# A decoder layer on one core: the stationary weights moved 64 bytes in SBUF, and side work reordered in the down projection and at the end

## The chip, the core and the metric

The kernel runs on one core of one Trainium2 chip. The metric is the device time of one execution in microseconds; the time before is the median of three runs, 2653.98 us (2652.39 to 2657.59).

## What is computed

One decoder layer, for 512 tokens of width 2048, in float32:

```python
q_a, k_a, v_a, q_b, k_b, v_b = jnp.split(h @ w_in[l], splits, axis=-1)
o_a = swa_sink_attention(q_a, k_a, v_a, sinks[l])      # sliding window of 128, 16 heads over 4
o_b = stick_breaking_attention(q_b, k_b, v_b)          # 16 heads, strictly causal
mix = jnp.concatenate([head_rmsnorm(o_a), head_rmsnorm(o_b)], axis=-1) @ w_o[l]
h = layer_norm(ALPHA * h + mix, ln1_g[l], ln1_b[l])
c = memory_cross_attention(h, mem, w_q_mem[l], w_kv_mem[l], w_o_mem[l])   # 4 heads, 256 keys
h = layer_norm(ALPHA * h + c, ln2_g[l], ln2_b[l])
gate, up = jnp.split(h @ w_gate_up[l], 2, axis=-1)     # 2048 -> 2 x 5632
f = (jax.nn.silu(gate) * up) @ w_down[l]
h = layer_norm(ALPHA * h + f, ln3_g[l], ln3_b[l])
```

## The kernel before, in words

**Products.** Each float32 operand is split into two float32r parts, hi and lo: ACT casts to hi (L123), DVE subtracts to get lo (L124). A product is three matmuls into the same accumulator: hi·hi, hi·lo, lo·hi (`mm3`, L144 to 149). A matmul loads its 128x128 stationary operand (PEld in the profile) while the one ahead of it streams its moving operand.

**Weights.** They come in units of 128x1024, 512 KB. `unit` (L135) loads one with a DMA on SP's queue into `ws` and splits it into `wh` and `wl`, three buffers each, in pool `pw`. `next_unit` (L683) keeps splits up to three units ahead of the product that uses them. In some stages the weights are the moving operand, with 512 columns (`v`, `wo`, `vo`, `pvo`, down); in others they are the stationary one: the attention's projections `pj..` (512 moving columns), and, with 256 moving columns, the memory's values `mvp` and keys `mkp` (`mem_project`), `kq` in the memory's attention, the early gate-up `ge`, and gate-up `zz` at L1055 (`product_turned`). Down is `zz` at L1044 (`product`).

In the built program every stationary and every moving operand of the float32r matmuls begins at the same place modulo 512 bytes. The one exception is the constant `bd`, which lies 352 bytes off that place (32 matmuls meet it: the 16 of L314 and L315 each, as the operand loaded next). The transposes are float32 and have the identity as moving operand.

**Gate-up and down** use a seven-product scheme for 2x2 blocks (Winograd's form of Strassen). A block runs through places 0 to 6, each with 2 to 4 groups; a group uses one unit. Three of the gate-up blocks are partial: part of their products was made early. The scheme's weight sums are made on DVE: `summed` adds a streamed tile to `a` or `b` (L600) and then splits it. `steps` (L575) writes the order of a block's loads and splits. Accumulators `zz` have three roles (`PRODUCTS`); places 0, 2, 4 and 6 add to the same one, and `end` (L1201) updates the four output quarters after each place. Hooks (`at_step`) put work ahead of a group.

**The end.** In the last block, `Last`, the normalisation of token tiles 0 and 1 is side work, run between the groups of the last places (`side.run`); tiles 2 and 3 follow after the loop, L1370. `shared` quarters of them go to ACT and POOL (L763 to 766), the others to DVE (L768, L770).

**Order.** PE's and SP's order is that of the code. DVE, ACT and POOL are ordered by a scheduling pass over the whole program, where `urgent` raises an operation's priority. All queues run in order.

Of the kernel before, what the change touches and what calls it, by code (L numbers as in the profile page):

```python
# [47 lines left out]
LOADS = 2  # L48
SIDE4 = 4
# [14 lines left out]
def layer(ctx, tc, io, out):  # L64
# [8 lines left out]
    pg = ctx.enter_context(tc.tile_pool(name="pg", bufs=4))  # L73
    pw = ctx.enter_context(tc.tile_pool(name="pw", bufs=3))
# [46 lines left out]

    def split(hi, lo, src):
        nc.scalar.copy(hi, src)  # L123
        return nc.vector.tensor_tensor(lo, src, f32(hi), op=ALU.subtract)  # L124
# [17 lines left out]
    latest = [None]  # L142
# [27 lines left out]
    dmt = const.tile([P, 2, 256], F32, name="dmt")  # L170
# [27 lines left out]
    for nb in range(2):  # L198
        acc = four_banks(nb, f"v{nb}")
        for u in range(8):  # L200
            if nb == 0 and u == 0:
                st, ws = pw.tile([P, 2, 512], F32, tag="ws", name="x0s"), pw.tile([P, 1024], F32, tag="ws", name="wvb0s")
                w = pw.tile([P, 1024], F32R, tag="wh", name="wvb0h"), pw.tile([P, 1024], F32R, tag="wl", name="wvb0l")
# [185 lines left out]
    class Window:  # L389
# [6 lines left out]
        def scores(self):  # L396
# [9 lines left out]
            for h in range(2):  # L406
                dist = dmt if st == 0 else dmt[:, 1:2].to_broadcast([P, 2, 256])
                slope = 2.0 ** (-8.0 * (a_head(j, h) + 1) / 16)
                nc.vector.scalar_tensor_tensor(
                    s[:, h].rearrange("p (b n) -> p b n", b=2), dist, -float(np.float32(slope)),  # L410
                    z[:, h].rearrange("p (b n) -> p b n", b=2), op0=ALU.mult, op1=ALU.add)
# [139 lines left out]
    def coming():  # L551
# [22 lines left out]
    def steps(name, src, groups, partial, first_half_early):  # L574

        a, b = {}, {}

# [15 lines left out]
        def hilo(src_):  # L593
            hi = pw.tile([P, 1024], F32R, tag="wh", name=f"{name}h")
            lo = pw.tile([P, 1024], F32R, tag="wl", name=f"{name}l")
            latest[0] = split(hi, lo, src_).ins
            return hi, lo

        def add(dst, x):
            nc.vector.tensor_tensor(dst, dst, x, op=ALU.add)  # L600

# [6 lines left out]
        def plain(x, g, then=None):  # L608
            def f():
                w = hilo(x[g])  # L610
                if then:
                    add(then[g], x[g])
# [13 lines left out]
        if first_half_early:  # L626
            for g in every:
                yield [load(streamed[2], st_tile, 2, g)], plain(streamed[2], g)
        for g in every:
            yield [load(b, b_tile, 3, g)] if partial else [], summed(a, b, g)  # L630
# [819 lines left out]
```

## Time and profile before

| | before |
|---|---|
| median of 3 runs | 2653.98 us |
| profiled execution | 2657.68 us |
| its span, first to last instruction | 2655.9 us |
| PE / PEld busy | 97% / 88% |
| DVE / ACT / POOL busy | 72% / 45% / 7% |
| mean granted TensorE clock | 0.992 |
| chain that ended last | PE 75%, issue 12%, DVE 5%, DMA 4% |

The span is what the profile covers; the rest of the execution's time, 1.8 us, lies around it. Busy time counts instructions in flight. Matmuls overlap, so a PE that is 100% busy says only that it never stood still; how fast it goes is read from the starts of successive matmuls. The chain that ended last is followed back from the last instruction, at each step to what released it.

### The profile page before, as it was taken

The page shows a single profiled execution, that of the slowest core. Times are in us where ns is not written, and L with a number is a line of the kernel's source. Part 1 is how long each engine was busy: PE and PEld are TensorE (multiplying, and loading weights), DVE is VectorE, ACT ScalarE, POOL GpSimd, SP SyncE. Part 2 cuts the span into 40 slices and gives each one's busy share as a digit, 9 for nine tenths or more (in the row PEclk, how much of TensorE's full clock was granted, in tenths as well). Part 3 has the DMA queues.
Part 4 walks back from the last instruction along what each step waited for, and adds up shares of the span by engine and source line. Part 5 has one row for each costly group of instructions (what it writes and reads, how often), then busy time and mean ns, then how long its engine had stood idle before and what let it go on. Part 6 is the DMA issues. An engine that isn't in the chain of part 4 may idle for free.

```text
span 2655.9 us, 40755 instructions
## 1 busy us (share of the span) xinstructions
PE 2588.7 (97%) x16544; PEld 2329.7 (88%) x16544; DVE 1914.3 (72%) x2170; ACT 1193.5 (45%) x1576; POOL 185.7 (7%) x324
## 2 busy tenths in 40 slices
PE   9999999999999999999999999999999998999995
PEld 7877777799988889988999999999999996877884
DVE  4258888997533574448797879887887777777788
ACT  3246656665421353334554444444445443333332
POOL 0001111010000000000000101010111001000001
PEclk9999999999999999999999999999999998999998
DMA  5322222245652483236755656563455577787763
GB/s 183 102 87 70 71 71 76 88 158 185 227 183 95 166 278 135 93 121 203 235 190 188 230 203 226 184 247 134 163 207 198 198 258 271 265 331 267 257 244 121
DMA packets 134747, 478.59 MB, mean 180 GB/s; under 512 B 16544, under 2 KB 16800, under 8 KB 133920
## 3 DMA queue, kind: packets, MB, share of 16 engines
q1 hardware_dynamic: 111024, 393.15, 42.8%
q0 software_dynamic: 23536, 82.85, 8.3%
q8 instruction: 129, 2.11, 0.3%
q14 instruction: 58, 0.48, 0.1%
HBM read 403.06 MB, written 72.88 MB: 179 GB/s over the span
## 4 chain that ended last, share of the span: by engine, by line
PE 75%; issue 12%; DVE 5%; DMA 4%; ACT 2%; POOL 1%; SPq 0%; POOLq 0%; DVEq 0%; ACTq 0%
PE zz L1055 20%; PE zz L1044 11%; PE mvp L147 1%; PE pjkb L147 1%; PE mvp L149 1%; PE mkp L149 1%; PE mkp L148 1%; PE mkp L147 1%; PE kq L149 1%; PE kq L148 1%; PE mvp L148 1%; PE kq L147 1%; PE pjqa L147 1%; PE pjkb L148 1%; PE vo L149 1%
## 5 line engine op out<-in xcount | busy, mean ns | idle before, releaser
L123 ACT CAST dn_1h<-dn_1a 128x1024 fp32r<-128x1024 f32 x44 | 46.4, 1055 | 82.5 <-PE zz L1044 73.6
L123 ACT CAST dn_0h<-dn_0a 128x1024 fp32r<-128x1024 f32 x44 | 46.0, 1052 | 77.7 <-PE zz L1044 40.6
L124 DVE TENSOR_TENSOR dn_0l<-dn_0a,dn_0h 128x1024 fp32r<-128x1024 f32 x44 | 53.4, 1220 | 21.2 <-ACT dn_0h L123 21.0
L124 DVE TENSOR_TENSOR dn_1l<-dn_1a,dn_1h 128x1024 fp32r<-128x1024 f32 x44 | 53.4, 1219 | 20.2 <-ACT dn_1h L123 20.2
L352 DVE TENSOR_TENSOR_SCAN a<-ones,nl 128x128 f32<-128x128 f32 (+3 forms) x64 | 49.8, 811 | 10.1 <-POOL nl L349 9.9
L1164 POOL DMA_DIRECT2D f_d<-fha x33 | 17.9, 542 | 407.9 <-ACT fha L123 407.5
L349 POOL TENSOR_SCALAR_AFFINE_SELECT nl<-nl 128x256 f32<-128x256 f32 x32 | 19.9, 621 | 344.3 <-DVE nl L348 344.3
L123 ACT CAST dn_0h<-dn_0b 128x1024 fp32r<-128x1024 f32 x22 | 23.2, 1054 | 45.9 <-PE zz L1044 41.5
L355 ACT ACTIVATE a<-a 128x256 f32<-128x256 f32 (+3 forms) x32 | 23.7, 739 | 38.8 <-DVE a L354 38.8
L123 ACT CAST dn_1h<-dn_1b 128x1024 fp32r<-128x1024 f32 x22 | 23.2, 1056 | 35.4 <-PE zz L1044 35.4
L421 ACT ACTIVATE sa<-sa,nm 128x256 f32<-128x256 f32 x64 | 31.9, 501 | 11.9 <-DVE nm L419 11.8
L147 PE MATMUL mvp<-mh,wmv_1h 128*128 128x256 f32 x128 | 37.1, 290 | 0.0
L600 DVE TENSOR_TENSOR dn_0a<-dn_0a,dn_0s 128x1024 f32<-128x1024 f32 x22 | 26.7, 1220 | 14.3 <-DMA dn_0s<-in_w_dn 14.2
L147 PE MATMUL mvp<-mh,wmv_0h 128*128 128x256 f32 x128 | 36.9, 288 | 0.0
L124 DVE TENSOR_TENSOR wmk_0l<-wmk_0s,wmk_0h 128x1024 fp32r<-128x1024 f32 x16 | 19.6, 1225 | 23.9 <-ACT wmk_0h L123 21.7
L149 PE MATMUL mvp<-mh,wmv_0l 128*128 128x256 f32 x128 | 36.3, 283 | 0.0
L147 PE MATMUL mkp<-mh,wmk_0h 128*128 128x256 f32 x128 | 36.2, 283 | 0.0
L148 PE MATMUL mkp<-ml,wmk_0h 128*128 128x256 f32 x128 | 36.2, 283 | 0.0
L149 PE MATMUL mkp<-mh,wmk_0l 128*128 128x256 f32 x128 | 36.2, 283 | 0.0
L147 PE MATMUL mkp<-mh,wmk_1h 128*128 128x256 f32 x128 | 36.2, 283 | 0.0
L148 PE MATMUL mkp<-ml,wmk_1h 128*128 128x256 f32 x128 | 36.2, 283 | 0.0
L149 PE MATMUL mkp<-mh,wmk_1l 128*128 128x256 f32 x128 | 36.2, 283 | 0.0
(2461 smaller groups left out, 10933.8 us busy)
## 6 DMA issues: line engine op xcount, KB each, us to landing
dn_1s<-in_w_dn SPq DMA_DIRECT2D x36, 512.0 KB, 4.7
dn_0s<-in_w_dn SPq DMA_DIRECT2D x33, 512.0 KB, 10.1
f_d<-fhs POOLq DMA_DIRECT2D x44, 256.0 KB, 2.7
f_d<-fls POOLq DMA_DIRECT2D x44, 256.0 KB, 2.9
f_d<-fha POOLq DMA_DIRECT2D x33, 256.0 KB, 5.6
f_d<-fla POOLq DMA_DIRECT2D x33, 256.0 KB, 4.8
wmv_0s<-in_w_mv SPq DMA_DIRECT2D x16, 512.0 KB, 3.4
wmv_1s<-in_w_mv SPq DMA_DIRECT2D x16, 512.0 KB, 3.3
```

The source lines that it names most:

```text
L123: nc.scalar.copy(hi, src)
L124: return nc.vector.tensor_tensor(lo, src, f32(hi), op=ALU.subtract)
L147: nc.tensor.matmul(acc, lh, rh, start=first, stop=False)
L148: nc.tensor.matmul(acc, lh, rl, start=False, stop=False)
L149: nc.tensor.matmul(acc, ll, rh, start=False, stop=last)
L349: nc.gpsimd.affine_select(out=nlt[:, :, dg], in_=nlt[:, :, dg], compare_op=ALU.is_gt, fill=0.0, base=0, channel_multiplier=1, pattern=[[0, ...
L352: nc.vector.tensor_tensor_scan(a[:, h, :nk][:, ::-1], ones.to_broadcast([P, nk]), nlt[:, h, :nk][:, ::-1], 0.0, op0=ALU.mult, op1=ALU.add)
L355: nc.scalar.activation(a[:, :, :nk], a[:, :, :nk], AF.Exp)
L421: nc.scalar.activation(s4[:, i], s4[:, i], AF.Exp, bias=nm[:, i:i + 1], accum_out=rs[:, i:i + 1])
L600: nc.vector.tensor_tensor(dst, dst, x, op=ALU.add)
L1044: nc.tensor.matmul(acc[:, t], l[:, cs(t, P)], r, start=first and c == 0 and i == 0, stop=last and c == 1 and i == 2, skip_group_check=True)
L1055: nc.tensor.matmul(z[:, j], l[:, cs(j, P)], r, start=first and c == 0 and i == 0 and j % 2 == 0, stop=last and c == 1 and i == 2, skip_gro ...
```

## The change

- A unit's hi and lo become the two halves of one tile of 2,064 float32 (`weight_pair`), of three pools with one buffer each. With `shift` both halves begin 16 floats, 64 bytes, later. The shift is given where weights are stationary and 256 columns move: `mem_project`, `kq`, the early gate-up, and gate-up. All else stays unshifted.
- Between the three pools stand two that hold the `bn` statistics, so that the three tiles begin at the same place modulo 256 bytes. `dmt` is stored in 384 columns instead of 512, and the window scores read it in two halves where `st` is 0.
- In the built program, 9,696 matmuls have stationary weights that begin 64 bytes (or 320) past the place of the moving operand, modulo 512. The others keep 0 (or 256).
- In the first down block, the update of `y12` with place 2's accumulator moves from the end of place 2 to place 3, that of `y22` from the arrival of its tile to place 4, and a load moves from 4 to 4.75.
- In the last block, four quarters of weight sums are no longer made by DVE from loaded tiles: after `b` has been split, accumulating DMAs on POOL's queue add the next blocks to `b` and `a` in place (`add_to`).
- In the last place of the last block, tile 2 is updated, measured and queued for normalisation as soon as its half is done; `shared` shrinks from (2,3) and (3,) to none and (3,). Side work of gate-up and down is ordered behind the latest cast on ACT (`behind_weights`).

```diff
+SHIFT = 16
...
+    pair_pools, stat_pools = [], []
+    for k in range(3):
+        pair_pools.append(ctx.enter_context(tc.tile_pool(name=f"pp{k}", bufs=1)))
+        if k < 2:
+            stat_pools.append(ctx.enter_context(tc.tile_pool(name=f"sp{k}", bufs=2)))
     pw = ctx.enter_context(tc.tile_pool(name="pw", bufs=3))
...
+    def weight_pair(name, shift=0):
+
+        pair_pools.append(pair_pools.pop(0))
+        w = pair_pools[-1].tile([P, 2048 + SHIFT], F32R, tag="w", name=f"{name}w")
+        return [w[:, k * 1024 + shift:][:, :1024] for k in range(2)]
+
-    def unit(src, name):
+    def unit(src, name, shift=0):
         st = stage(src, name)
-        hi = pw.tile([P, 1024], F32R, tag="wh", name=f"{name}h")
-        lo = pw.tile([P, 1024], F32R, tag="wl", name=f"{name}l")
+        hi, lo = weight_pair(name, shift)
         latest[0] = split(hi, lo, st).ins
         return hi, lo
...
-                w = unit(src[o, u], f"w{name}{o}_{u}")
+                w = unit(src[o, u], f"w{name}{o}_{u}", SHIFT)
...
-                    yield io["w_mq"][h, i2], f"wmq{h}_{i2}"
+                    yield io["w_mq"][h, i2], f"wmq{h}_{i2}", SHIFT
...
-                    yield io["w_gu"][n, b, g], f"wge{n}_{b}_{g}"
+                    yield io["w_gu"][n, b, g], f"wge{n}_{b}_{g}", SHIFT
...
+        shift = SHIFT if name.startswith("gu") else 0
...
+        def add_to(tiles, blk, g):
+            return lambda: nc.gpsimd.dma_start(tiles[g], src(blk, g), accum_op=ALU.add)
...
+        if last:
+            for g in every:
+                yield [], plain(b, g, add_to(b, 1, g), add_to(a, 2, g))
+            for g in every:
+                yield [], plain(b, g)
+            for g in every:
+                yield [], plain(a, g)
+            return
...
-                if self.e5 is not None:
-                    self.update(self.y22, self.e5, True, ALU.subtract)
...
                 at_step(self.i, 2.85, rest)
-                at_step(self.i, 4, last_quad)
+                at_step(self.i, 3.6, lambda: self.update(self.y12, self.held, True, ALU.subtract))
+                at_step(self.i, 4.25, lambda: self.update(self.y22, self.e5, True, ALU.subtract))
+                at_step(self.i, 4.75, last_quad)
...
+            elif place == 2 and self.i == len(gu_order):
+                self.held = acc
...
+    def behind_weights(n):
+        if side.todo:
+            with tc.issue_after(latest[1]):
+                side.run(n)
...
                 for t in range(2):
                     for g in range(groups):
                         product(z, name, g, ws[g], False, g == groups - 1, (t,))
-                        side.run(SIDE4)
+                        behind_weights(SIDE4)
+                    urgent(tt, kind.y21[:, t], kind.y21[:, t], z[:, t], op=ALU.add)
+                    final[2 + t, 1] = kind.y21[:, t]
+                    urgent(bn, "n3", 2 + t, 1)
+                    side.add(normalised(2 + t, {0: (), 1: (3,)}[t]))
...
     side.drain()
-    for t in range(2, NT):
-        for _ in normalised(t, {2: (2, 3), 3: (3,)}[t]):
-            pass
```

PE's order is the same in both programs. Three places of the others follow, in each the rows before the change and then the rows after it. The changed file's line numbers differ: its L131, L132, L136, L620, L798 and L800 are L123, L124, L128, L600, L768 and L770 of before.

DVE in the first down block, around the first two updates of `yu` (`y12` and `y22`; `e` is the saved accumulator of place 1, `zz_0` that of place 2; `dn_0l` or `dn_0w` the weights' lo):

```order
L124 TENSOR_TENSOR dn_0l<-dn_0b_21583,dn_0h 128x1024
L600 TENSOR_TENSOR dn_0b_21583<-dn_0b_21583,dn_0s_21863 128x1024
L124 TENSOR_TENSOR dn_0l<-dn_0b_21609,dn_0h 128x1024
L600 TENSOR_TENSOR dn_0b_21609<-dn_0b_21609,dn_0s_21881 128x1024
L128 SCALAR_TENSOR_TENSOR yu_21822<-yu_21822,e_21753 128x1024
L128 SCALAR_TENSOR_TENSOR yu_21822<-yu_21822,zz_0_21557 128x1024
L124 TENSOR_TENSOR dn_0l<-dn_0b_21636,dn_0h 128x1024
L124 TENSOR_TENSOR dn_0l<-dn_0b_21560,dn_0h 128x1024
```

```order
L132 TENSOR_TENSOR dn_0w<-dn_0b_21039,dn_0w 128x1024
L620 TENSOR_TENSOR dn_0b_21039<-dn_0b_21039,dn_0s_21305 128x1024
L132 TENSOR_TENSOR dn_0w<-dn_0b_21064,dn_0w 128x1024
L620 TENSOR_TENSOR dn_0b_21064<-dn_0b_21064,dn_0s_21323 128x1024
L136 SCALAR_TENSOR_TENSOR yu_21268<-yu_21268,zz_0_21014 128x1024
L136 SCALAR_TENSOR_TENSOR yu_21268<-yu_21268,e_21202 128x1024
L132 TENSOR_TENSOR dn_0w<-dn_0b_21090,dn_0w 128x1024
L132 TENSOR_TENSOR dn_0w<-dn_0b_21017,dn_0w 128x1024
```

The two updates have changed places with each other, and nothing else has moved.

DVE in the last place of the last block, from the second weight subtraction on (`n3st` and `n3mv` are the last normalisation's statistics, `dn_1a` the weights of that place):

```order
L124 TENSOR_TENSOR dn_1l<-dn_1a_24176,dn_1h 128x1024
L704 BN_STATS n3st_24117<-yq_11_24075 128x6
L704 BN_STATS n3st_24119<-yq_11_24075 128x6
L770 SCALAR_TENSOR_TENSOR yq_00_23798<-yq_00_23798,n3mv_24546,ln_b_24499 128x512
L770 SCALAR_TENSOR_TENSOR yq_00_24069<-yq_00_24069,n3mv_24546,ln_b_24499 128x512
L770 SCALAR_TENSOR_TENSOR yu_23802<-yu_23802,n3mv_24546,ln_b_24500 128x512
L770 SCALAR_TENSOR_TENSOR yq_10_24073<-yq_10_24073,n3mv_24546,ln_b_24500 128x512
L743 BN_AGGR n3mv_24602<-n3st_24044 128x2
L600 TENSOR_TENSOR dn_1a_24194<-dn_1a_24194,dn_1s_24558 128x1024
L745 TENSOR_SCALAR n3mv_24602<-n3mv_24602 128x1
L768 SCALAR_TENSOR_TENSOR yq_00_23798<-yq_00_23798,n3mv_24602,ln_g_24497 128x512
L768 SCALAR_TENSOR_TENSOR yq_00_24069<-yq_00_24069,n3mv_24602,ln_g_24497 128x512
```

```order
L132 TENSOR_TENSOR dn_1w<-dn_1a_23503,dn_1w 128x1024
L800 SCALAR_TENSOR_TENSOR yq_10_23405<-yq_10_23405,n3mv_23846,ln_b_23808 128x512
L773 BN_AGGR n3mv_23896<-n3st_23377 128x2
L132 TENSOR_TENSOR dn_1w<-dn_1a_23520,dn_1w 128x1024
L775 TENSOR_SCALAR n3mv_23896<-n3mv_23896 128x1
L798 SCALAR_TENSOR_TENSOR yq_00_23143<-yq_00_23143,n3mv_23896,ln_g_23805 128x512
L778 SCALAR_TENSOR_TENSOR n3mv_23896<-n3mv_23896 128x1
L798 SCALAR_TENSOR_TENSOR yq_00_23401<-yq_00_23401,n3mv_23896,ln_g_23805 128x512
L136 TENSOR_TENSOR yq_01_23403<-yq_01_23403,zz_0_23559 128x512
```

The add at L600 is gone, the third subtraction stands two operations after the second instead of behind the add and five normalising steps, and tile 2's last update stands among the normalising steps of tile 1.

POOL at its end (`y_d` is scratch for the outputs' quarters):

```order
L1244 DMA yq_01_24071<-y_d 128x1024
L1244 DMA yq_10_24073<-y_d 128x1024
L757 TENSOR_SCALAR neg_24678<-n3mv_24670 128x1
L757 TENSOR_SCALAR neg_24704<-n3mv_24696 128x1
L764 TENSOR_TENSOR yu_23802<-yu_23802,ln_g_24498 128x512
L764 TENSOR_TENSOR yq_11_24075<-yq_11_24075,ln_g_24498 128x512 x2
L766 TENSOR_TENSOR yu_23802<-yu_23802,ln_b_24500 128x512
L766 TENSOR_TENSOR yq_11_24075<-yq_11_24075,ln_b_24500 128x512 x2
```

```order
L1275 DMA yq_10_23405<-y_d 128x1024
L623 DMA dn_1a_23483<-in_w_dn 128x1024
L623 DMA dn_1a_23503<-in_w_dn 128x1024
L623 DMA dn_1a_23520<-in_w_dn 128x1024
L623 DMA dn_1b_23539<-in_w_dn 128x1024
L623 DMA dn_1b_23562<-in_w_dn 128x1024
L623 DMA dn_1b_23581<-in_w_dn 128x1024
L787 TENSOR_SCALAR neg_23990<-n3mv_23982 128x1
L794 TENSOR_TENSOR yq_11_23407<-yq_11_23407,ln_g_23806 128x512
L796 TENSOR_TENSOR yq_11_23407<-yq_11_23407,ln_b_23808 128x512
```

Six accumulating transfers have come (and six loads have left SP's queue), and four of six products have gone to DVE.

## Rows read from the trace of the kernel before

**Rows 1.** The page: engines' busy time; granted clock by slice; a group (busy, mean ns).

```profile
PE 2588.7 (97%) x16544; PEld 2329.7 (88%) x16544; DVE 1914.3 (72%) x2170; ACT 1193.5 (45%) x1576; POOL 185.7 (7%) x324
...
PEclk9999999999999999999999999999999998999998
...
L124 DVE TENSOR_TENSOR dn_1l<-dn_1a,dn_1h 128x1024 fp32r<-128x1024 f32 x44 | 53.4, 1219 | 20.2 <-ACT dn_1h L123 20.2
```

**Rows 2.** Stretches (us): length, busy of PE, PEld, DVE, ACT, POOL; clock, DMA.

```profile
500.00:600.00 100.00, 98.10 (x744) 89.97 (x743) 92.24 (x134) 66.28 (x121) 11.77 (x14) 1.00 0.41 135
...
1600.00:1700.00 100.00, 98.52 (x817) 97.94 (x817) 86.72 (x84) 46.23 (x50) 11.02 (x21) 1.00 0.55 190
1900.00:2000.00 100.00, 100.00 (x836) 100.00 (x835) 78.60 (x74) 46.58 (x49) 7.59 (x14) 1.00 0.43 154
...
2626.00:2635.00 9.00, 8.27 (x24) 6.08 (x24) 5.80 (x11) 0.40 (x3) 0.00 (x0) 0.66 0.35 117
```

**Rows 3.** Timeline of PE in gate-up: start us, us, what; the first and 19th.

```profile
1899.75 0.28 PE L1055 MATMUL zz<-s4h,gu7h 128*128 128x256 f32 x1
...
1901.91 0.28 PE L1055 MATMUL zz<-s4h,gu7h 128*128 128x256 f32 x1
```

**Rows 4.** Timeline of PE in down: the first and 11th.

```profile
2289.70 0.39 PE L1044 MATMUL zz<-dn_1l,s1h 128*128 128x512 f32 x1
...
2291.97 0.39 PE L1044 MATMUL zz<-dn_1h,s1l 128*128 128x512 f32 x1
```

**Rows 5.** Single lines and tiles: duration ns min/median/max, first and last start.

```profile
L1055 PE MATMUL zz<-a11l,gu3h x32: 282/283/283, 1356.1 to 1367.2; 128*128 128x256 f32 x32
...
L1044 PE MATMUL zz<-dn_0h,s2l x44: 389/389/389, 2208.2 to 2534.1; 128*128 128x512 f32 x44
...
L147 PE MATMUL avb<-pbh,vbh x80: 277/282/287, 158.4 to 601.9; 128*128 128x256 f32 x80
...
L371 PE MATMUL trb<-ident,a x160: 270/272/331, 150.4 to 593.5; 128*128 128x128 f32 x160
...
L409 DVE SCALAR_TENSOR_TENSOR sa<-dmt,za x32: 659/677/687, 179.7 to 591.4; 128x512 f32<-128x512 f32 x32
```

**Rows 6.** Timeline of DVE, first down block; in brackets its idle time and releaser.

```profile
2230.35 1.23 DVE L128 SCALAR_TENSOR_TENSOR yu<-yu,e 128x1024 f32<-128x1024 f32 x1 [7.89 <-DMA yu<-y_d]
```

**Rows 7.** PE's waits from 2180 to 2260: total us, times, longest.

```profile
PE zz L1044 <- DVE dn_0l L124: 8.5, 2, 6.7
```

**Rows 8.** PE's waits from 2600 to the end.

```profile
PE zz L1044 <- ACT dn_1h L123: 4.3, 1, 4.3
...
PE zz L1044 <- DVE dn_1l L124: 0.6, 1, 0.6
```

**Rows 9.** Timeline of DVE at the end.

```profile
2616.72 0.74 DVE L768 SCALAR_TENSOR_TENSOR yq<-yq,n3mv,ln_g 128x512 f32<-128x512 f32 x1
...
2623.80 1.16 DVE L600 TENSOR_TENSOR dn_1a<-dn_1a,dn_1s 128x1024 f32<-128x1024 f32 x1
...
2635.22 1.28 DVE L128 TENSOR_TENSOR yq<-yq,zz 128x512 f32<-128x512 f32 x2 [3.39 <-PE zz L1044]
...
2642.10 1.83 DVE L768 SCALAR_TENSOR_TENSOR yq<-yq,n3mv,ln_g 128x512 f32<-128x512 f32 x1
...
2649.69 1.75 DVE L770 SCALAR_TENSOR_TENSOR yu<-yu,n3mv,ln_b 128x512 f32<-128x512 f32 x1
```

**Rows 10.** Tile `yq`, its loads of 512 KB from POOL's queue.

```profile
DMA to landing us min/median/max: 2.4/6.9/13.1
```

**Rows 11.** Timeline of PE around `bd`, the operand that lies elsewhere.

```profile
538.30 0.28 PE L149 MATMUL mvp<-mh,wmv_0l 128*128 128x256 f32 x1
...
538.42 0.39 PE L314 MATMUL ms<-sq,bd 128*128 128x512 f32 x1
...
538.65 0.40 PE L315 MATMUL ms<-sq,bd 128*128 128x512 f32 x1
...
538.88 0.28 PE L147 MATMUL mvp<-mh,wmv_0h 128*128 128x256 f32 x1
```

More of the change, by code (lines that the diff above doesn't have):

```diff
@@ L169, in layer @@
     ident = const.tile([P, P], F32, name="ident")
-    dmt = const.tile([P, 2, 256], F32, name="dmt")
+    dmt = const.tile([P, 384], F32, name="dmt")
     bd = const.tile([P, P], F32R, name="bd")
@@ L406, in scores @@
             for h in range(2):
-                dist = dmt if st == 0 else dmt[:, 1:2].to_broadcast([P, 2, 256])
                 slope = 2.0 ** (-8.0 * (a_head(j, h) + 1) / 16)
-                nc.vector.scalar_tensor_tensor(
-                    s[:, h].rearrange("p (b n) -> p b n", b=2), dist, -float(np.float32(slope)),
-                    z[:, h].rearrange("p (b n) -> p b n", b=2), op0=ALU.mult, op1=ALU.add)
+                s2, z2 = (v[:, h].rearrange("p (b n) -> p b n", b=2) for v in (s, z))
+                whole = dmt[:, :256].unsqueeze(1)
+                if st == 0:
+                    nc.vector.scalar_tensor_tensor(s2[:, 0], dmt[:, 128:], -float(np.float32(slope)), z2[:, 0],
+                                                   op0=ALU.mult, op1=ALU.add)
+                    nc.vector.scalar_tensor_tensor(s2[:, 1], dmt[:, :256], -float(np.float32(slope)), z2[:, 1],
+                                                   op0=ALU.mult, op1=ALU.add)
+                else:
+                    nc.vector.scalar_tensor_tensor(s2, whole.to_broadcast([P, 2, 256]), -float(np.float32(slope)), z2,
+                                                   op0=ALU.mult, op1=ALU.add)
             mx = sm.tile([P, 4], F32, tag="mx", name=f"mx{j}_{st}")
@@ L571, in coming, with steps @@
                 for g in range(4):
-                    yield io["w_gu"][n, b, g], f"wge{n}_{b}_{g}"
-    def steps(name, src, groups, partial, first_half_early):
+                    yield io["w_gu"][n, b, g], f"wge{n}_{b}_{g}", SHIFT
+    def steps(name, src, groups, partial, last):
         a, b = {}, {}
+        shift = SHIFT if name.startswith("gu") else 0
         def load(tiles, make, blk, g):
@@ L593, in hilo @@
         def hilo(src_):
-            hi = pw.tile([P, 1024], F32R, tag="wh", name=f"{name}h")
-            lo = pw.tile([P, 1024], F32R, tag="wl", name=f"{name}l")
+            hi, lo = weight_pair(name, shift)
             latest[0] = split(hi, lo, src_).ins
+            latest[1] = casts[-1]
             return hi, lo
@@ L606, in summed, with plain @@
             return f
-        def plain(x, g, then=None):
+        def plain(x, g, *then):
             def f():
                 w = hilo(x[g])
-                if then:
-                    add(then[g], x[g])
+                for h in then:
+                    h()
                 return w
@@ L630, in steps @@
             yield [load(b, b_tile, 3, g)] if partial else [], summed(a, b, g)
+        if last:
+            for g in every:
[5 more added lines that the diff above has]
+            return
         for g in every:
@@ L634, in steps @@
             yield [load(streamed[1], st_tile, 1, g)], summed(b, streamed[1], g)
-        if partial or first_half_early:
-            streamed[2] = {}
+        if partial:
             for g in every:
@@ L640, in steps @@
             for g in every:
-                yield [load(streamed[2], st_tile, 2, g)], plain(streamed[2], g, then=a)
+                yield [load(streamed[2], st_tile, 2, g)], plain(streamed[2], g, lambda g=g: add(a[g], streamed[2][g]))
             for g in every:
@@ L702, in bn @@
         if (name, t) not in stats:
-            stats[name, t] = sm.tile([P, 4, 6], F32, tag="bst", name=f"{name}st{t}", bufs=4)
+            stats[name, t] = stat_pools[t // 2].tile([P, 4, 6], F32, tag="bst", name=f"{name}st{t}")
         nc.vector.bn_stats(stats[name, t][:, nb], ycol(t, nb))
@@ L1227, in end @@
             elif place == 6:
-                for t in range(2) if self.last else (slice(0, 2),):
-                    self.update(self.y21[:, t], acc[:, t], True, ALU.add)
+                self.update(self.y21, acc, True, ALU.add)
                 self.done(self.y21, 0, 1)
@@ L1360, in layer @@
                         z, name, g, next_unit(), fresh and g == 0, g == groups - 1)
-                    side.run(SIDE4)
-            kind.end(place, z)
+                    behind_weights(SIDE4)
+                kind.end(place, z)
             if kind is last and place == 2:
```

10 lines of the change are left out of this document (5 added, 5 removed).

## The prediction

> **What bounds the kernel now.** I read the page first, then a table of stretches, then single matmuls. TensorE (PE) is busy for 97% of the span at a granted clock of 1.00 nearly throughout, which is the 2.4 GHz level [rows 1]. By stretch it is 100% busy in the projections of the memory and in gate-up, and the others only come near: VectorE (DVE) reaches 92% beside attention, 87% in the gate-up blocks that hold partial sums, 79% in the others [rows 2]. So what matters is how long one matmul takes, and there are two prices. In gate-up (256 moving columns) 18 periods run from 1899.75 to 1901.91: 120 ns each [rows 3]. In down (512 columns) 10 periods run from 2289.70 to 2291.97: 227 ns each [rows 4]. The 256 columns between them cost 107 ns, so 120 = 107 + 13 and 227 = 213 + 13: each matmul carries a fixed 13 ns, whatever its width. That is what the shift can reach. 13 ns is also the time in which 32 columns stream.
>
> The Trainium skill, TensorE: Matmul & The Clock Gate, section Back-to-back issue gap, gives a warm spacing of N/2.4 + 2.5 ns, which would be 109 and 216 ns. The trace differs by 11 ns in both widths, and the measurement decides.
>
> **The shift.** The order of the matmuls does not change, only their addresses. 9,696 matmuls get stationary weights 64 bytes further on, modulo 128: 768 each for the memory's values and keys and for kq, 576 early gate-up, 1,440 in three partial blocks and 5,376 in eight full ones. All have 256 columns. No row shows this offset, so I bound it. A recorded duration is its period plus 163 ns (283 against 120; 389 against 227, plus 162). Above: the shortest period that contains a weight load of 128 columns is that of the transposes, 272 − 163 = 109 ns [rows 5], 11 ns under 120; all of it would give 9,696 × 11 = 107 us. Below: the attention's value matmuls, of the same width and with both operands where they always are, spread from 277 to 287 [rows 5], so 114 to 124 ns: they start behind wider matmuls, so loads and streams meet at other moments. That a fixed offset changes those moments for good is the theory; 124 would cost 9,696 × 4 = 39 us. I take the short end of the nearest row, of the same width and type: 114 ns, a gain of 6 ns. Where DVE is already at 87 to 92% (1,440 partial gate-up matmuls and the 768 of the memory's values) I count half, because there a faster PE meets a late split [rows 2]. (9,696 − 1,104) × 6 = **51.6 us**.
>
> **What goes with the shift** costs nothing. A shared tile is free again one matmul later than its first half was (120 to 227 ns); three tiles rotate, so two units, over 5 us, cover cast and subtraction (1.2 us each at most [rows 1]). Cutting sixteen of the window's 128x512 operations in two adds sixteen on DVE, at most 16 × 0.68 = 11 us of it [rows 5], in a stage where it has that room and PE has other matmuls. The bn tiles only move.
>
> **The first down block.** DVE waits 7.9 us for `yu` [rows 6], and PE 6.7 us for the subtraction queued behind that [rows 7]. The new hooks are written later in the program. But the changed DVE order has the two `yu` updates at the same place, ahead of the same two subtractions, merely swapped: whichever is first waits for the same transfer. I take 0; the bounds are 0 and 10 us, the wait and some three us of slower clock behind it.
>
> **The end.** Six adds leave DVE (6 × 1.2 = 7.2 us) and six transfers move from SP to POOL as accumulating ones. Before, PE waited 4.3 us for a cast whose add stood behind the normalisation, at 2623.80 [rows 8, 9], then 0.6 us for its subtraction, and then ran at half clock (0.66 mean) until 2635 [rows 2]. Now the cast needs only its transfer, but the subtractions still stand between normalising steps. Walking the new DVE order with the old durations from 2609 puts them at 2623.0 and 25.0, and PE ends near 2631.5 instead of 2635: 3.5 us. After that DVE worked from 2635.22 to 2651.44, 16.2 us [rows 9]; the new order leaves about 12 of it, since one half of the last two tiles is added while PE runs the other, and two POOL products stand where six did. Beside those a 0.74 us step took up to 1.83 [rows 9], so I add 2 back: 2.5 us gained. Sum **6 us**, bounds −4 and 10. The lower end is the new wait: an accumulated tile is needed some 8 us after its issue; 512 KB loads from POOL took 2.4 to 13.1 us, 6.9 in the middle [rows 10]. If the slowest came first, some 4 us would be lost on PE, and the cast that waits on ACT would hold the statistics behind it.
>
> The new ordering edge after the cast orders ACT alone, and only side work at the end; it is in the walk. The SP queue loses six loads and its output issues move up: 0, as DVE ends later.
>
> **Sum.** The profiled execution took 2657.68 us, 1.8 outside its span of 2655.9. 2657.7 − 51.6 − 6 = 2600.1. The median of the runs shown, 2653.98, is 3.7 under the profiled one: **2596 us**.
>
> **The rivals.**
> *Nothing but the end.* The fixed 13 ns may be the change of weights itself, no collision. For it: it is the same for 256 and 512 columns [rows 3, 4], and one operand already lies elsewhere: the 32 matmuls around the stationary `bd` meet it 352 bytes off. The one ahead of it keeps 120 ns (538.30 to 538.42), and the next take 0.23 us [rows 11], no less than 227. Against it: 352 is not a multiple of 64, and single matmuls between two kinds say little of a steady stream. It gives 2657.7 − 6 − 3.7 = 2648. The Trainium skill speaks for this rival: TensorE: Matmul & The Clock Gate, section Step-by-step, says that PE has two independent read ports, so loading the next weights takes no read bandwidth from the running matmul. The stream with its 13 ns neither shows nor excludes that.
> *All of it.* If load and stream now never meet, 109 ns as in the transposes: 107 us less some 10 in the DVE-heavy blocks, and the 6: 2551.
> *Slower.* The shift holds loads and streams in the worse meeting of the two, 124 ns [rows 5], in all 9,696: + 39, − 6: 2687. It decides as soon as a steady gate-up period is over 120.6 ns, where 6 us are used up. For it: the spread goes both ways. Against it: in most value matmuls the period is 119 or less.
>
> **How the numbers follow.** The forecast, some gain between 110 and 119 ns, gets 0.50; all of it 0.12; nothing but the end 0.25; slower 0.13. The range takes in the first three: from 2545, the full price with the end's better bound, to 2654, no gain from the shift and the end's lower bound nearly used up. A measurement of this kernel can tell about 0.2%, 5 us, from no change: under 2648.7 is faster. The rival with the end alone lies on that line, so half of it is faster, half the same: 0.62 + 0.12 = 0.74 faster, 0.13 the same, 0.13 slower.
>
> **What would show it.** In gate-up, 100 us should hold some 875 matmuls, not 836, and durations near 277, not 283; in down 227 ns should stay, as nothing shifts there. DVE should be over 90% busy in the partial blocks. The wait for `yu` should stay near 8 us. At the end the wait for the cast should be gone, with two shorter ones for subtractions, and last matmul and end 4 and 6 us closer to the last down block's start. Wrong: 836 matmuls again (then the first rival), 917 (the second), under 830 (the third); or a PE wait at the end that a POOL transfer ends.

## The result

The changed kernel took **2621.12 us** (median of 4 runs, 2619.38 to 2628.31), the kernel before 2654.22 us (2652.39 to 2657.59): a ratio of 0.9877, 95% interval 0.9865 to 0.9889. 2596 was forecast, in a range from 2545 to 2654. The direction was right, and some 57% of the gain came: 33 of 58 us.

The profiled executions took 2657.68 and 2628.31 us, with spans of 2655.9 and 2626.4. The page of the changed kernel, with the group of weight subtractions:

```profile
PE 2555.2 (97%) x16544; PEld 2294.9 (87%) x16544; DVE 1907.0 (73%) x2183; ACT 1189.8 (45%) x1572; POOL 186.9 (7%) x325
...
PEclk9999999999999999999999999999999999999998
...
L132 DVE TENSOR_TENSOR dn_1w<-dn_1a,dn_1w 128x1024 fp32r<-128x1024 f32 x44 | 53.5, 1219 | 20.8 <-ACT dn_1w L131 20.8
```

PE is 33.5 us less busy with the same 16,544 matmuls [rows 1], and the granted clock is nearly the same (0.992 and 0.993 in the mean): the matmuls themselves have become shorter, by 1.3%. The stretches tell which ones (columns as in rows 2):

```profile
500.00:600.00 100.00, 97.62 (x759) 89.87 (x758) 92.66 (x138) 66.96 (x122) 11.29 (x14) 1.00 0.42 143
1516.00:1566.00 50.00, 50.00 (x443) 50.00 (x443) 39.41 (x36) 23.41 (x24) 1.62 (x3) 1.00 0.51 184
1600.00:1700.00 100.00, 98.51 (x860) 97.71 (x859) 87.97 (x83) 47.18 (x50) 8.41 (x16) 1.00 0.54 194
1900.00:2000.00 100.00, 100.00 (x851) 100.00 (x851) 77.15 (x72) 48.76 (x51) 8.11 (x15) 1.00 0.48 173
```

100 us of gate-up hold 851 matmuls from 1900 on, where 836 stood [rows 2] and 875 were expected; but 50 us from 1516 on hold 443, which is 886 in 100 us. Both stretches are without a wait, at the same clock, and made of the same kind of instructions. There are **two prices**, called levels from here on: a level is the mean period of a stretch of matmuls without a wait, and the periods of such a stretch are called even. Single matmuls of PE's timeline show them, the first and the 19th of such a stretch at each:

```profile
1530.00 0.39 PE L1085 MATMUL zz<-s3h,gu4w 128*128 128x256 f32 x2
...
1532.04 0.39 PE L1085 MATMUL zz<-s3h,gu4w 128*128 128x256 f32 x2
```

```profile
1900.05 0.40 PE L1085 MATMUL zz<-a12h,gu7w 128*128 128x256 f32 x2
...
1902.17 0.40 PE L1085 MATMUL zz<-a12h,gu7w 128*128 128x256 f32 x2
```

18 periods in 2.04 us are 113.3 ns each; 18 in 2.12 us are 117.8; before it was 120 [rows 3]. (Periods here and below are differences of starts in the trace.) On the whole 9,552 shifted matmuls that follow one another without a wait gained 38.0 us, 4.0 ns each.

Against that stand longer waits of PE in the part of gate-up that holds the blocks with partial sums (1320 to 1745), where it waits for the weights' subtractions and casts:

```profile
PE zz L1085 <- DVE gu1w L132: 3.4, 3, 2.1
PE zz L1085 <- DVE gu2w L132: 3.1, 4, 1.8
PE zz L1085 <- DVE gu0w L132: 2.6, 3, 1.4
PE zz L1085 <- DVE gu3w L132: 2.4, 3, 1.5
```

These four are 11.5 us; the same four waits before (from 1330 to 1760) are 3.4 us:

```profile
PE zz L1055 <- DVE gu1l L124: 1.2, 3, 0.6
PE zz L1055 <- DVE gu0l L124: 1.1, 3, 0.6
PE zz L1055 <- DVE gu2l L124: 0.7, 2, 0.6
PE zz L1055 <- DVE gu3l L124: 0.4, 1, 0.4
```

The first down block still waits for its transfer, and the end has changed (waits of PE from 2580 on, then DVE):

```profile
2207.77 1.22 DVE L136 SCALAR_TENSOR_TENSOR yu<-yu,zz 128x1024 f32<-128x1024 f32 x1 [7.71 <-DMA yu<-y_d]
```

```profile
PE zz L1074 <- DVE yq L136: 4.2, 1, 4.2
PE zz L1074 <- DVE n3mv L779: 0.8, 1, 0.8
```

```profile
2594.51 1.21 DVE L136 TENSOR_TENSOR yq<-yq,zz 128x1024 f32<-128x1024 f32 x1
...
2608.13 0.68 DVE L136 TENSOR_TENSOR yq<-yq,zz 128x512 f32<-128x512 f32 x1
...
2620.25 1.75 DVE L800 SCALAR_TENSOR_TENSOR yu<-yu,n3mv,ln_b 128x512 f32<-128x512 f32 x1
```

DVE's wait for `yu` is 7.7 us [rows 6: 7.9]. The 4.3 us for a cast [rows 8] is replaced by 4.2 us for an update that frees an accumulator. From DVE's update with the last sum to its last operation's start there are 12.1 us, where 14.5 stood [rows 9].

Since PE's order is the same in both programs, the start of each matmul can be compared with its own before. Of the 29.5 us between the spans, 20.9 come in the shifted matmuls (38.0 of shorter periods, 17.1 given back, nearly all of it in longer waits), 6.3 elsewhere on PE, 2.3 in the tail behind it. By stage:

| stage, shifted matmuls | forecast us | measured us |
|---|---|---|
| memory's values, 768 | 2.3 | 2.6 |
| memory's keys, 768 | 4.6 | 1.7 |
| kq, 768 | 4.6 | 3.0 |
| early gate-up, 576 | 3.5 | 2.8 |
| partial blocks, 1,440 | 4.3 | -3.8 |
| full blocks, 5,376 | 32.3 | 14.5 |

### The profile page after: what moved, and what is told of

Same layout as the page of the kernel before. It is cut to its first block, busy times and chain, and to the rows that moved or that the text cites. A ratio compares the mean times of both kernels' runs of the same rounds, so it can differ in the third digit from the quotient of the medians.

```text
span 2626.4 us, 40562 instructions
## 1 busy us (share of the span) xinstructions
PE 2555.2 (97%) x16544; PEld 2294.9 (87%) x16544; DVE 1907.0 (73%) x2183; ACT 1189.8 (45%) x1572; POOL 186.9 (7%) x325
## 2 busy tenths in 40 slices
DMA packets 134746, 478.52 MB, mean 182 GB/s; under 512 B 16544, under 2 KB 16928, under 8 KB 133920
## 4 chain that ended last, share of the span: by engine, by line
issue 41%; PE 40%; DVE 9%; DMA 4%; ACT 3%; POOL 3%; SPq 0%; POOLq 0%; DVEq 0%; ACTq 0%
PE zz L1085 16%; PE zz L1074 11%; DVE a L365 1%; POOL f_d L1194 1%; DMA dn_0s<-in_w_dn 1%; PE mvp L160 1%; PE mvp L162 1%; PE mvp L161 1%; DVE a L367 1%; PE pjqa L160 1%; PE pjqa L162 1%; PE pjqa L161 1%; DMA s3r<-f_d 1%; DVE dn_0w L132 0%; DVE pbl L132 0%
## 5 line engine op out<-in xcount | busy, mean ns | idle before, releaser
L131 ACT CAST dn_0w<-dn_0a 128x1024 fp32r<-128x1024 f32 x44 | 46.0, 1052 | 74.3 <-PE zz L1074 45.8
L131 ACT CAST dn_1w<-dn_1a 128x1024 fp32r<-128x1024 f32 x44 | 46.4, 1054 | 68.8 <-PE zz L1074 67.1
L132 DVE TENSOR_TENSOR dn_0w<-dn_0a,dn_0w 128x1024 fp32r<-128x1024 f32 x44 | 53.3, 1221 | 21.1 <-ACT dn_0w L131 21.0
L132 DVE TENSOR_TENSOR dn_1w<-dn_1a,dn_1w 128x1024 fp32r<-128x1024 f32 x44 | 53.5, 1219 | 20.8 <-ACT dn_1w L131 20.8
L131 ACT CAST fhs<-f 128x512 fp32r<-128x512 f32 x44 | 27.3, 621 | 37.1 <-DVE f L1003 26.0
L131 ACT CAST dn_0w<-dn_0b 128x1024 fp32r<-128x1024 f32 x22 | 23.2, 1054 | 45.1 <-PE zz L1074 39.6
L131 ACT CAST dn_1w<-dn_1b 128x1024 fp32r<-128x1024 f32 x22 | 23.2, 1055 | 37.9 <-PE zz L1074 31.8
L160 PE MATMUL mvp<-mh,wmv_1w 128*128 128x256 f32 x128 | 36.8, 288 | 0.0
L160 PE MATMUL mvp<-mh,wmv_0w 128*128 128x256 f32 x128 | 36.5, 285 | 0.0
L162 PE MATMUL mkp<-mh,wmk_0w 128*128 128x256 f32 x128 | 36.0, 282 | 0.0
L160 PE MATMUL mkp<-mh,wmk_1w 128*128 128x256 f32 x128 | 36.0, 282 | 0.0
L161 PE MATMUL mkp<-ml,wmk_1w 128*128 128x256 f32 x128 | 36.0, 282 | 0.0
L162 PE MATMUL mkp<-mh,wmk_1w 128*128 128x256 f32 x128 | 36.0, 281 | 0.0
L161 PE MATMUL mkp<-ml,wmk_0w 128*128 128x256 f32 x128 | 36.0, 281 | 0.0
L160 PE MATMUL mkp<-mh,wmk_0w 128*128 128x256 f32 x128 | 36.0, 281 | 0.0
L162 PE MATMUL mvp<-mh,wmv_0w 128*128 128x256 f32 x128 | 35.9, 280 | 0.0
```

The lines of the kernel that those rows point to most:

```text
L131: casts[:] = [nc.scalar.copy(hi, src).ins]
L160: nc.tensor.matmul(acc, lh, rh, start=first, stop=False)
L161: nc.tensor.matmul(acc, lh, rl, start=False, stop=False)
L162: nc.tensor.matmul(acc, ll, rh, start=False, stop=last)
```

## The experiments

All are the changed kernel with one edit, unless said otherwise. The kernel before took 2654.76 us beside e1 to e4, 2656.57 beside e5 to e8, 2656.39 beside e9 to e11 and 2655.76 beside e12.

### Is it the 64 bytes: e1

```diff
-SHIFT = 16
+SHIFT = 0
-        w = pair_pools[-1].tile([P, 2048 + SHIFT], ...
+        w = pair_pools[-1].tile([P, 2064], ...
```

> The changed kernel with the shift set to 0; tiles, pools and order of side work stay. Theory (the 64 bytes buy the time): steady 256-column periods go back to 120 ns (836 per 100 us in gate-up), the extra PE waits in the partial blocks go away with them (17.1 us), so 2621.1 + 38.0 - 17.1 = 2642 us, 12 under the kernel before. Rival (the new tiles and the order of side work buy it, the shift nothing): periods stay at 117.8 and 113.3 ns and the time at 2621.

It took 2651.55 us (2649.95 to 2653.43), ratio to before 0.9988 (0.9980 to 0.9997). Two of its stretches:

```profile
1516.00:1566.00 50.00, 50.00 (x419) 50.00 (x418) 38.85 (x38) 22.51 (x24) 4.33 (x8) 1.00 0.32 114
1900.00:2000.00 100.00, 100.00 (x835) 100.00 (x835) 79.27 (x74) 46.09 (x48) 7.57 (x14) 1.00 0.44 160
```

This is 3 us under the kernel before on the same chip, where the changed kernel is 33 under it: the shift makes the gain, 30 us of the 33. That is 9 us more than I expected, since I had worked from the profiled execution, which at 2628.3 is the slowest of four, and had let all of the 17.1 us of waits go with the shift. They do not: the matmuls that ran from 1300 to 1800 us before take 504.3 us here against 499.9, with the same 120 ns a matmul, so 4.4 us are lost without any shift. The new tiles or the new order may cost them; e10 looks into it. So of the 17.1 us given back, only some 13 go with the shift.

### Which offset: e2, e4, e6, e7

```diff
-SHIFT = 16
+SHIFT = 8 (e2), 12 (e6), 24 (e7), 32 (e4)
...
```

Not shown here: e2 and e6 keep the tile at 2,064 float32; in e7 and e4 the tile grows with the shift, and e7 also moves two statistics tiles.

> The changed kernel with a shift of 32 bytes, half of it, in tiles of the same size. Theory (an offset has to reach a step of 64 bytes to help): 120 ns as with none, 2642 us. Rival (every byte of offset counts in proportion): periods half way, about 119 and 116.7 ns, 2631. Rival (any offset but 0 does): 117.8 and 113.3 ns again, 2621.

> The changed kernel with a shift of 128 bytes and tiles 64 bytes longer, so that the three tiles start at different places: the 256-column matmuls fall into three classes, 3,264 at 128 bytes, 3,216 at 192 bytes and the rest at 0 modulo 256, and 512-column ones into 0, 64, 128 and 192. Theory (an offset of 64 bytes or more modulo 256 helps): 113.3 or 117.8 ns at 128 and 192, 120 at 0, so two thirds of the gain: 2621 + 21 / 3 = 2628, less what 512 columns gain at 64 to 192. Rival (only 64 bytes help, 128 falls on the same place again): 120 ns at 0 and 128, 2635.

> Shift of 48 bytes in tiles of the same size. Measured so far: 120 ns at 0, 118.3 at 32 bytes, 113.3 or 117.8 at 64. If the gain grows with the offset up to 64 bytes: some 116 ns on one level, 2628. If 64 bytes is a step: 118.3 as at 32 bytes, 2638.

> Shift of 96 bytes; the tiles are 32 bytes longer, and two of the four statistics tiles move to another pool so that the three tiles start 8,448 bytes apart as in the changed kernel. If the gain falls again beyond 64 bytes (128 bytes gave 118.4): some 116 to 118 ns, 2625 to 2638. If 64 bytes lies at the edge of a better range: 113.3 ns or less on one level, 2590 to 2600.

Levels at 256 columns, between neighbours of the same offset (at 48 bytes 117 and 130 ns in turn make 123.3):

| offset modulo 256, bytes | ns | whole kernel us (range) |
|---|---|---|
| 0 (e1) | 120.0 | 2651.6 (2650.0 to 2653.4) |
| 32 (e2) | 118.3, one level | 2638.3 (2636.2 to 2640.0) |
| 48 (e6) | 117.8, 118.3 and 123.3 | 2645.2 (2639.5 to 2659.8) |
| 64 (changed kernel) | 113.3 and 117.8 | 2621.1 (2619.4 to 2628.3) |
| 96 (e7) | 117.3 and 118.7, in 3% 120.0 | 2636.2 (2634.7 to 2640.4) |
| 128 (e4) | 118.7 | 2652.8 in all (2650.8 to 2654.6) |
| 192 (e4) | 117.8 | |

None of the simple rules holds: not that any offset but 0 gives the levels of 64 bytes, not a gain in proportion, not a step at 64 bytes. Every offset but 0 has levels below 120, and 64 bytes has the best of those tried. At 48 bytes, two stretches without a wait in one execution:

```profile
1516.00:1566.00 50.00, 50.00 (x407) 50.00 (x407) 36.66 (x34) 22.57 (x23) 2.42 (x5) 1.00 0.34 122
1900.00:1950.00 50.00, 50.00 (x426) 50.00 (x426) 37.45 (x35) 23.80 (x25) 3.24 (x6) 1.00 0.54 201
```

407 matmuls in 50 us is slower than the 419 of no shift (e1). So the rival "slower" exists, at 123.3 ns; it only does not come at the changed kernel's offset in any of the executions seen. The times of e4 say little about the offset, as its 512-column matmuls moved too (next).

### Why moving weights stay where they are: e3

```diff
-    def weight_pair(name, shift=0):
+    def weight_pair(name, shift=SHIFT):
-    def unit(src, name, shift=0):
+    def unit(src, name, shift=SHIFT):
-        shift = SHIFT if name.startswith("gu") else 0
+        shift = SHIFT
```

> The changed kernel with all weights shifted by 64 bytes, moving ones too, so that 5,016 matmuls of 512 columns have an offset of 64 or 192 bytes modulo 256. Theory (the offset counts whichever operand lies later): their period falls from 226.7 ns to 220 (as 120 to 113.3) or 224.4 (as 120 to 117.8), 33 or 11 us less, 2588 to 2610. Rival (512 columns gain nothing, their 13 ns is the change of weights): 226.7 ns and 2621.

It took 2629.92 us (2622.36 to 2635.71). In down the weights are the moving operand, so that the stationary one now begins 64 bytes ahead of it, 192 modulo 256. Down, with the row of the changed kernel first and that of e3 second, the same stretch:

```profile
2430.00:2480.00 50.00, 50.00 (x222) 41.45 (x221) 36.25 (x31) 18.99 (x18) 2.12 (x4) 1.00 0.61 208
```

```profile
2430.00:2480.00 50.00, 50.00 (x220) 41.05 (x219) 34.31 (x29) 19.51 (x19) 2.67 (x5) 1.00 0.65 229
```

With 512 columns the offset lengthens the period: in down from 226.9 to 229.9 ns, in `wo` from 226.7 to 233.3, and in the attention's projections, where the stationary weights moved and the offset is 64 bytes, from 230.8 to 233.3. Both theories were wrong in the sign. Over all 5,016 some 17 us are lost (an estimate from the periods by stage); the whole kernel is only 9 us longer. Its gate-up held the faster level more often (77% of the even periods in the profiled execution, 45% in the first of the changed kernel), which makes up for part of the loss. So what an offset does has to be measured for each width.

This run also tells whether the distance of the two operands counts or the place of the stationary one. In attention's values `vaa` and `vab` 256 columns of weights move, and the stationary operand stayed where it was. The first and the 19th matmul, before and then in e3:

```profile
100.29 0.28 PE L147 MATMUL vaa<-wva0h,xh 128*128 128x256 f32 x1
...
102.45 0.28 PE L147 MATMUL vaa<-wva1h,xh 128*128 128x256 f32 x1
```

```profile
100.91 0.28 PE L160 MATMUL vaa<-wva0w,xh 128*128 128x256 f32 x1
...
103.03 0.28 PE L160 MATMUL vaa<-wva1w,xh 128*128 128x256 f32 x1
```

120.0 ns have become 117.8, which is what 192 bytes gave in e4, where the stationary operand had moved. And in e4 itself the matmuls of `vaa` and `vab` at 128 bytes go through the same periods of 115, 118, 121, 120 and 119 ns in turn as the shifted ones at 128 bytes. So it is the distance, as far as these two show it.

### Does a level belong to a place: e5

No edit.

> The changed kernel as it is, once more. Theory (at 64 bytes there are two levels, 113.3 and 117.8 ns a matmul; which one holds is drawn anew when PE restarts after a wait, and stays until the next): the levels stand in other stretches than in the first profile, the eight full gate-up blocks (5,376 matmuls, at 117.8 then) somewhere between 113.3 and 117.8, and the times of its runs scatter by up to 5,376 x 4.5 ns = 24 us, 2598 to 2630. Rival (the level belongs to the place in the program, by its addresses): 113.3 up to the last partial block and 117.8 in all full ones again, and times within some 8 us as so far.

2623.72 us (2620.24 to 2624.29). The same two stretches in the first profile and in this one:

```profile
1365.00:1415.00 50.00, 50.00 (x443) 50.00 (x442) 37.66 (x33) 22.79 (x22) 0.00 (x0) 1.00 0.24 84
1800.00:1850.00 50.00, 50.00 (x427) 50.00 (x426) 37.18 (x33) 23.46 (x24) 1.62 (x3) 1.00 0.47 166
```

```profile
1365.00:1415.00 50.00, 50.00 (x427) 50.00 (x426) 35.79 (x31) 20.83 (x21) 0.00 (x0) 1.00 0.21 72
1800.00:1850.00 50.00, 50.00 (x443) 50.00 (x443) 39.18 (x35) 23.55 (x25) 2.71 (x5) 1.00 0.51 188
```

Nearly the same instructions, at the same addresses, stand at 113.3 in one execution and at 117.8 in the other, and the other way round in the second stretch: the level does not belong to the place. The times scattered far less than the theory allowed. In the traces of the first execution, e3 and e5 each change of level inside gate-up stands right behind an interval of over 125 ns; in the first execution the last such change is here:

```profile
1739.42 0.36 PE L1085 MATMUL zz<-s3h,gu2w 128*128 128x256 f32 x1 [0.48 <-DVE f L136]
1739.62 0.28 PE L1085 MATMUL zz<-s3l,gu2w 128*128 128x256 f32 x1
1740.46 0.50 PE L1085 MATMUL zz<-s3h,gu2w 128*128 128x256 f32 x2 [0.57 <-DVE gu2w L132]
```

Before it 113.3 held, after it 117.8, and from there to 2158 no wait of PE is listed: 417 us at the slower level. (Two longer intervals at 1788, of 134 and 226 ns, left it as it was, so not every break changes it.) This also says why the slower level lasts. At 113.3 ns PE catches up with the side work and waits now and then, which sets the level anew; at 117.8 it does not. (That reading is an argument; the next run tests its first half.)

### Does a break in the stream set the level: e9

In each unit of the full blocks one matmul is issued as two halves, without a wait:

```diff
+                    if nudge and (c, j, i) == (1, 0, 0):
+                        for k in range(2):
+                            nc.tensor.matmul(z[:, j, cs(k, P)], l[:, cs(j, P)], r[:, cs(k, P)], ...)
+                        continue
```

> The changed kernel; in each of the 224 units of the eight full gate-up blocks one matmul of 256 columns is issued as two of 128 (same operands and sums), which breaks the even stream without any wait. Theory (the level of 113.3 or 117.8 ns is a phase between weight load and stream that any break in the stream sets anew): the full blocks no longer hold one level for hundreds of us; it changes at these matmuls, or all units take the level that this break leads to: at 113.3 up to 5,152 x 4.5 = 23 us less in matmuls, 224 x 15 to 30 ns = 3 to 7 us more for the break; 2600 to 2625. Rival (the level follows something else, data transfers or VectorE's reads): long stretches of 117.8 as before, and 3 to 7 us more, about 2628.

2631.82 us (2631.39 to 2637.04). Behind a split the periods start at 117 to 120 ns and come down to 113.3 within some five matmuls. Ahead of 208 of the 224 splits stand ten even periods, the end of the unit before, and in all 208 they are at 113.3. One split in PE's timeline:

```profile
2007.50 0.28 PE L1090 MATMUL zz<-a11h,gu9w 128*128 128x256 f32 x1
2007.61 0.33 PE L1087 MATMUL zz<-a11h,gu9w 128*128 128x128 f32 x2
2007.78 0.33 PE L1090 MATMUL zz<-a11l,gu9w 128*128 128x256 f32 x1
2007.95 0.40 PE L1090 MATMUL zz<-a11h,gu9w 128*128 128x256 f32 x2
```

So a break without a wait sets the level, and a break of this kind sets the faster one: that is shown. That the level is a phase between weight load and stream is how I read it; no run shows the phase itself. My price for the break was wrong. From 2007.61 to 2007.95 the split and the next matmul take 0.34 us where two periods are 0.23: 0.11 us, 224 of them 25 us. That takes more than the level gives: in the first profile 3,376 matmuls of the full blocks stood at 117.8, and 4.5 ns less for each would be 15 us.

### Do the shared tiles cost anything: e10

```diff
-        w = pair_pools[-1].tile([P, 2048 + SHIFT], F32R, tag="w", name=f"{name}w")
-        return [w[:, k * 1024 + shift:][:, :1024] for k in range(2)]
+        return [pw.tile([P, 1024], F32R, tag=f"w{k}", name=f"{name}{k}") for k in "hl"]
-            stats[name, t] = stat_pools[t // 2].tile([P, 4, 6], F32, tag="bst", name=f"{name}st{t}")
+            stats[name, t] = sm.tile([P, 4, 6], F32, tag="bst", name=f"{name}st{t}", bufs=4)
```

> The changed kernel with hi and lo in tiles of their own, as before the change, and the statistics in one pool as before; so no shift either. To be held against the run with the shift at 0 (2651.6 us; from 1300 to 1800 us it lost 4.4 us against the kernel before, in waits of PE for weights' subtractions and casts). Theory (a shared tile is handed back later, and that is what makes these waits longer): the 4.4 us come back, 2647. Rival (it is the changed order of the side work or chance): the stretch stays as long, 2651.

2650.68 us (2649.21 to 2653.63) against 2651.55: between the two expectations, and not to be told apart by time. By the traces gate-up, first matmul to last, is 904.2 us before, 908.6 in e1 and 905.9 here, all at 120 ns, so 2.7 of e1's 4.4 us are not there with separate tiles. That is one execution of each, and it shows no cause: in four executions with the same gate-up code (the changed kernel, e5, e8 and e11) the matmuls that ran from 1300 to 1800 before take 490.5 to 493.0 us, a spread of 2.5. What the 4.4 us are stays open.

### The wait for yu: e8

```diff
+            def late(y_, acc):
+                with tc.issue_after(latest[0]):
+                    self.update(y_, acc, True, ALU.subtract)
-                at_step(self.i, 3.6, lambda: self.update(self.y12, self.held, True, ALU.subtract))
-                at_step(self.i, 4.25, lambda: self.update(self.y22, self.e5, True, ALU.subtract))
+                at_step(self.i, 3.8, lambda: late(self.y12, self.held))
+                at_step(self.i, 4.25, lambda: late(self.y22, self.e5))
```

> The changed kernel, and in the first down block the two updates of yu are ordered behind the weight subtractions already issued, which puts two subtractions ahead of the first update and four ahead of the second. Theory (PE's 6.7 us there is the subtraction queued behind the wait for yu's transfer, and some 3 us more go to the lower clock after it): the wait goes, 7 to 10 us less than the changed kernel's run on the same chip, apart from the scatter of the levels; stretch from the first down matmul to the end shorter by as much. Rival (PE then waits for something else of the same transfer, the accumulator that the update frees): the wait moves a few us later and nothing is gained.

2617.44 us (2613.28 to 2621.24), ratio to before 0.9856 (0.9839 to 0.9872), against 2623.72 for the changed kernel on the same chip. DVE waits less for `yu` (7.71 us in the changed kernel):

```profile
2201.99 1.22 DVE L136 SCALAR_TENSOR_TENSOR yu<-yu,zz 128x1024 f32<-128x1024 f32 x1 [3.77 <-DMA yu<-y_d]
```

PE's waits from 2160 to 2260, first in the changed kernel and then in e8:

```profile
PE zz L1074 <- DVE dn_0w L132: 8.8, 3, 6.5
```

```profile
PE zz L1074 <- DVE dn_0w L132: 3.2, 2, 1.7
PE zz L1074 <- ACT dn_0w L131: 2.0, 1, 2.0
```

The wait of 6.5 us is gone, one of 2.0 us has taken part of its place, and from the last gate-up matmul to the last of all 441.5 us pass, where 448.9 and 448.2 did in the two executions of the changed kernel: 7 us.

### What sets the end: e11

From e8; the side steps of the last two groups of place 4 are written behind its update:

```diff
-                    behind_weights(SIDE4)
+                    if not (kind is last and place == 4 and g >= groups - 2):
+                        behind_weights(SIDE4)
```

> The kernel with the late yu updates, and in the last block, before the last place, the eight side steps of the last two groups are written after the update of place 4 and not before it, so that VectorE frees the accumulator that PE waits 4.3 us for. Theory (the end is set by VectorE, which works without a gap from there to the last operation): PE ends some 3 us earlier, the tail after it grows by nearly as much, and the time stays within 1 us of 2617. Rival (PE sets the end, VectorE has slack): 3 us less, 2614.

2615.94 us (2609.31 to 2621.05), 1.5 us under e8 with ranges that overlap. PE's last part is 1.6 us shorter than in e8 (439.9 against 441.5), and the tail behind PE grew from 18.4 to 20.8 us: no gain that shows. PE's wait is not even gone, 4.0 us. DVE sets the end: in the changed kernel it is busy for all of 2590 to 2610, while PE has 12.4 us of work:

```profile
2590.00:2610.00 20.00, 12.41 (x44) 8.46 (x42) 19.97 (x37) 3.07 (x8) 0.00 (x0) 0.91 0.29 103
```

### All that helped: e12

From e11, with 20 split matmuls: in places 2 and 5 of each full block (`place in (2, 5) and g == 1`) and four in the memory's keys.

> The kernel with the late yu updates and the earlier accumulator update, and 20 split matmuls: two in each of the eight full gate-up blocks, in their third and sixth places, and four in the projection of the memory's keys. Measured: a split costs some 0.11 us and left the 113.3 ns level behind it in all 208 units where the level could be read. Theory (the level holds until the next wait): the keys run at 113.3 (768 x 4.5 = 3.4 us), the full blocks mostly so (in the runs without splits up to 260 us of them stood at 117.8, 2,200 x 4.5 = 10 us), less 2.2 us for the splits: 2604 to 2610, with less scatter. Rival (the faster matmuls only meet waits for VectorE in the same place): no less than 2614.

2612.64 us (2609.11 to 2615.94), ratio to before 0.9838 (0.9825 to 0.9852), the fastest of all. Gate-up:

```profile
1900.00:2000.00 100.00, 100.00 (x883) 99.91 (x883) 82.94 (x79) 52.17 (x56) 10.27 (x19) 1.00 0.60 220
```

883 matmuls: the level holds. 92% of gate-up's even periods stand at it, where the first profile has 45%, e8 53% and e11, without a split, 72%; and gate-up is 875.1 us long against 884.4 in e8 and 881.4 in e11. But the last part of PE grew to 446.7 us, with 10.8 us of PE's waits between 2140 and 2520, most of them for DVE's subtractions, where e8 has 8.9, and a granted clock of 0.98 from 2150 to 2580, where e8 has 1.00. So the 2604 to 2610 were not reached: gate-up gained 6 us on e11 and down lost 7 in these two executions. That the faster gate-up causes the loss is not shown; the granted clock of that stretch differs between executions, 0.98 in the first profile and 0.99 in e5 with the same program.

## Why the prediction was right, and where it was wrong

**What bounds the kernel**: right for 256 columns. Part of a matmul's period, beyond what its columns explain, could be had by moving an address, and 30 of the 33 us came from that (e1). That the shift can reach the same 13 ns at any width is wrong: at 512 columns the tried offsets only lengthened the period (e3). The formula of 109 and 216 ns beside it was read too widely. The Trainium skill, TensorE: Matmul & The Clock Gate, section Back-to-back issue gap, calls N/2.4 + 2.5 ns the gap of an isolated matmul and not that of a stream with weight loads. So the 11 ns by which the trace differs say nothing against it.

**The shift's price** is the term that was mis-sized: "I take the short end of the nearest row, of the same width and type: 114 ns." The faster level is that, 113.3. But a second level of 117.8 held for 63% of the full blocks: their shorter periods gave 20.5 us, of which 6.0 went into longer waits that the forecast had put at nothing there, so 14.5 us in place of 32.3. I had read the spread of 277 to 287 ns [rows 5] as a range to choose from; it could have been read as a sign that one and the same offset allows several periods.

**Blocks in which DVE is busy**: "I count half, because there a faster PE meets a late split." The mechanism was right, the half too mild: in the partial blocks the shorter periods gained 7.9 us and longer waits took 11.7. Part of these waits is not from the faster PE at all, which is the next step.

**"What goes with the shift costs nothing"** was wrong by the traces: 4.4 us more in gate-up at an unchanged 120 ns (e1). Whether the shared tiles or the new order cost them stays open (e10). "two units, over 5 us, cover cast and subtraction" left out that DVE serves other work in between, and PE already waited for these subtractions before, 3.4 us.

**The first down block**: right, the two updates wait 7.7 us for the same transfer as before. e8 shows that the cause was the one named, and what it was worth.

**The end**: 2.5 us were forecast for the tail and 2.4 came (20.8 to 18.4); for PE 3.5 were forecast and 1.5 came from 2600 on. The cast no longer waits there, but the update of an accumulator behind normalising steps takes over. I had the lower bound as a late POOL transfer; that came too, but only to ACT, 6.0 us in two waits:

```profile
ACT dn_1w L131 <- DMA dn_1b<-in_w_dn: 6.0, 2, 4.6
```

Not foreseen were 2.0 us between 2400 and 2500, where two waits of 1.2 us in all for `dn_1l` are gone, and 1.5 us between 300 and 400, where the granted clock was 0.98 and is 1.00. These 3.5 us are luck as far as the forecast goes: no term of it stands for them.

**The profiled execution against the median**: 3.7 us before, 7.2 after, which is why the medians lie 33 us apart and the profiles 29. The levels differ between executions (e5), so they are the likely reason.

**The rivals.** *Nothing but the end* fell: without the shift 2651.6, with it 2621. What spoke for it was a sentence of the Trainium skill, TensorE: Matmul & The Clock Gate, section Step-by-step, by which loading the next weights takes no SBUF read bandwidth from the running matmul. The traces show that the two operands are not independent all the same: with the same instructions in the same order the period depends on the distance of the two operands, from 113.3 ns (64 bytes) to 123.3 (48 bytes). The reason is not shown by any run; a collision of the two reads stays the likely one. *All of it* (a level of 109 ns) was seen nowhere. *Slower* was not this offset's, but it is real at 48 bytes, and for 512 columns at 64 and 192.

## What to carry to other kernels

Where PE is the bound, compare its period with what the columns explain, and try where stationary and moving operands begin; measure each offset for each width, since 64 bytes gained up to 6.7 ns at 256 columns and lost 2.5 at 512 (e3). Read such a gain in several executions and stretches, not from one row: it can come in levels that a wait sets anew. And when the engine that bounds a kernel gets faster, the limit shifts at once: of 38 us of shorter matmuls some 13 (17.1 less the 4.4 of e1) were given back by the shift, most of it in waits for VectorE's subtractions, so the work that makes PE's operands has to become faster with it.

## What the runs showed that was not expected

A matmul stream of equal instructions has more than one steady period, and at 64 bytes it changed only behind a wait or a break: 113.3 or 117.8 ns at 64 bytes, 117.8, 118.3 or 123.3 at 48 bytes, one of 120.0 at 0. In the first execution one choice lasted 417 us. Two halves of 128 columns in place of one matmul of 256 led to 113.3 in all 208 units that could be read, for 0.11 us each.
